# A hybrid trunk kernel: RWKV's first chunk issued at raised priority beside Mamba's end, raw weights fetched six slots ahead, two tables for the last token's shares

## The chip, the cores and the metric

The kernel runs on one core of a Trainium2 chip. The metric is the device time in microseconds (us). Several runs are timed; beside them one execution is profiled, and it has a time of its own. The engines are PE (TensorE, matrix products; PEld is its weight load), DVE (VectorE), ACT (ScalarE), POOL (GpSimd) and SP (SyncE, which here only issues DMA transfers). Each engine works through its own queue of instructions in a fixed order and waits on semaphores for the others.

## The reference

One layer over 4096 tokens of 1024 values: RMSNorm, one input projection, three groups of heads that read the same projection, one output projection, RMSNorm and the residual. The part that matters here:

```python
h = rmsnorm(x, pre_norm_w[i])
u = h @ w_in[i]
y_ssm  = mamba2_group(u[..., :SSM_IN], ...)                  # conv, SiLU, chunked scan, gate, norm
y_rwkv = rwkv7_group(u[..., SSM_IN:SSM_IN + RWKV_IN], ...)
y_mem  = memory_xattn_group(u[..., SSM_IN + RWKV_IN:], mem_k, mem_v)
y = jnp.concatenate([y_ssm, y_rwkv, y_mem], axis=-1)
x = x + rmsnorm(y @ w_out[i], post_norm_w[i])

# rwkv7_group begins with the token shift: each token takes a share of its predecessor
prev = jnp.pad(u, ((0, 0), (1, 0), (0, 0)))[:, :l, :]
us = u + (prev - u) * mu
# and its heads follow S_t = S_{t-1} (diag(w_t) + a_t^T b_t) + v_t^T k_t ; y_t = S_t r_t
```

## The kernel before, in words

The tokens are cut into 16 chunks of 256 (`NT`). The work has three phases. Phase A does the Mamba group for all chunks, phase B the RWKV group for all chunks, phase C attention and the output projection. The normalised input, transposed and split into a high and a low part (`hh`, `hl`), is written to DRAM in phase A and read again in B and C.

Every product of float32 quality is made of three matmuls on such parts: high by high, high by low, low by high. `proj_cm` (line 145) does it with the weights as the stationary operand, 24 matmuls for one block of 128 columns; a pair of blocks shares one PSUM tile `ps_pj`, of which there are two buffers. The weights are fetched raw (`fetch`, line 70, on SP's queue, into a tile `w_st`) and split by `split_w`: ACT writes `w_hi` (line 80), DVE writes `w_lo` (line 81). RWKV needs five weight blocks: the latent one `wlat` (128 columns), `wk`, `wr`, `wv` and `wg` (256 each), in four pieces each, so 20 fetches and 40 splits. `load_b` issues them, with two slots for the raw tiles.

In phase A one chunk has a stage 1 (projections, a causal convolution on DVE in `cc0` to `cc3`, lines 335 to 342) and a stage 2 (the scan in two halves: `R` holds the decays, which come back from DRAM as a broadcast, lines 386 to 438; `xdt`, `yd`, `st`, `prev`, `y`). The last chunk's stage 2 is called `a_tail`. It runs beside the beginning of phase B.

In phase B the stage 1 of a chunk calls `shifted` once for the latent block, k, r, v and g. `shifted` projects a pair of blocks into `ps_pj`, then ACT scales it by 1 - mu into `tt` (line 609), DVE adds mu times the predecessor for tokens 1 to 255 (line 610), POOL does token 0 with the table `cm`, which holds the share that the last chunk's last token left (line 612), and DVE writes the new share of this chunk's last token over it (line 613). Only after that is the PSUM buffer free for the next projection:

```python
g.tensor_tensor(out=us[:, :, 0], in0=tt[:, 0:nb, 0], in1=cm[:, m0:m0 + nb], op=ALU.add)
v.tensor_tensor(out=cm[:, m0:m0 + nb], in0=pv[:, :, NT - 1], in1=mu[:, m0:m0 + nb], op=ALU.mult)
```

The rest of stage 1 builds the products `AR` and `BK`: `lora` on the latent block (lines 642 and 643), the key norm (`norm`, line 676, with POOL's `rho`), `unit` (lines 695 to 710), `bonus` (lines 720 and 721). Then `gram2` (line 772) forms `AT`, `solve2` inverts small triangular blocks (lines 788 to 860, with `nct`, `N`, `T`, `Df`), `stage3` steps the state four times per chunk (lines 913 to 957: `UV`, `X`, `ST`, matmuls of lines 920, 927, 937), and `stage4` normalises.

What sets the order: the program is written as generators, and `weave` draws from several of them in turn, in proportion to given step counts. The result is the order of the program. The Tile framework then schedules it against a model of the engines (`schedule_with_timeline_sim=True`): instructions of a higher priority go first where they are ready, and what comes out is one fixed order per engine. The streams may be given a third number, with which `weave` issues their steps inside `tc.high_priority(offset=...)`. At the passage from A to B one line weaves the two streams:

```python
weave((a_tail, 10), (chain(load_b(), stage1(0, hT0, r0_)), 48))
```

Of the kernel before, what the change touches and what calls it, by code (L numbers as in the profile page):

```python
# [7 lines left out]
F32 = mybir.dt.float32  # L8
# [3 lines left out]
ALU = mybir.AluOpType  # L12
AX = mybir.AxisListType

P = 128
# [12 lines left out]
def tile_hymba_trunk(  # L28
# [59 lines left out]
    def load_w(src, c0, w, scale, stp, bufs=2, low=None):  # L88
        for kq in range(4):
            split_w(w, fetch(src, c0, w[0].shape[2], stp, kq, bufs), scale, kq, low)  # L90
            yield
# [443 lines left out]
    def phase_b(a_tail, a_l):  # L535
# [5 lines left out]
        ws_s = ExitStack()  # L541
        wsb = ws_s.enter_context(tc.tile_pool(name="wsb", bufs=2, side="right", reuse_waits="tile"))
        C = 64
# [5 lines left out]
        def load_b():  # L549
            for c_, w_ in ((1024, wlat), (256, wk), (0, wr), (512, wv), (768, wg)):  # L550
                yield from load_w(w2d, C_RW + c_, w_, pnc, wsb)

# [30 lines left out]
        v.memset(dcy, -0.5 * EXPM05)  # L583
        cm = bs.tile([P, 9], F32, name="cm")
        v.memset(cm, 0.0)

# [10 lines left out]
        def shifted(hT, ws, m0, nm, mid=None, pool=None, at=0, tag=None):  # L597
            wb = blocks(ws)
            nb = len(wb)
            pj = ps_pj()  # L600
            for b_ in range(nb):
# [6 lines left out]
            for b_ in range(nb):  # L608
                s.activation(out=tt[:, b_, :], in_=pv[:, b_, :], func=AF.Copy, scale=omu[:, m0 + b_:m0 + b_ + 1])
                v.scalar_tensor_tensor(out=us[:, b_, 1:NT], in0=pv[:, b_, 0:NT - 1], scalar=mu[:, m0 + b_:m0 + b_ + 1],  # L610
                                       in1=tt[:, b_, 1:NT], op0=ALU.mult, op1=ALU.add)
            g.tensor_tensor(out=us[:, :, 0], in0=tt[:, 0:nb, 0], in1=cm[:, m0:m0 + nb], op=ALU.add)
            v.tensor_tensor(out=cm[:, m0:m0 + nb], in0=pv[:, :, NT - 1], in1=mu[:, m0:m0 + nb], op=ALU.mult)  # L613
            return us
# [115 lines left out]
        r0_ = {}  # L730
        weave((a_tail, 10), (chain(load_b(), stage1(0, hT0, r0_)), 48))
        ws_s.close()
# [18 lines left out]
        v.scalar_tensor_tensor(out=amask, in0=amask, scalar=hsel[:, 1:2], in1=mk[:, 0:P], op0=ALU.max, op1=ALU.mult)  # L751
        nct = bi.tile([P, 16, 2 * NPC], F32, name="nct")
        pw = bi.tile([P, NPC, 32], F32, name="pw")
# [29 lines left out]
        def solve2(i, r):  # L783
            AT = r["AT"]
            for q in range(4):
                qs = slice(q * 32, q * 32 + 32)
                h, half = q // 2, q % 2
                s.copy(
                    out=nct[qs].rearrange("p t (c b) -> p c b t", b=2),
                    in_=AT[qs, :, h, half * 32:half * 32 + 32].rearrange("p c (b t) -> p c b t", b=2))  # L790
# [545 lines left out]
```

## Time and profile before

| | us |
|---|---|
| median of 3 runs | 2209.16 (2206.49 to 2212.63) |
| the profiled execution | 2211.41 |
| its span, first to last instruction | 2209.6 |
| PE busy | 2151.8 |
| DVE busy | 1502.7 |
| ACT busy | 1181.1 |
| POOL busy | 726.7 |
| mean granted clock of PE | 0.986 |

The span is some 1.8 us shorter than the execution's time. Busy time is the sum over an engine's instructions; matmuls are pipelined, so a busy PE is not PE at its peak. The granted clock says what share of full speed PE was given. A wait is put down to the instruction that ended last before the waiting one began. Phase A ends and phase B begins at about 740 to 800 us of the span.

### The profile page before, as it was taken

How to read it: one execution, taken by the hardware profiler on the slowest of the kernel's cores; microseconds unless marked ns; L12 is line 12 of the kernel's file. 1: busy time of each engine (PE TensorE's matmuls, PEld its weight loads, DVE VectorE, ACT ScalarE, POOL GpSimd, SP SyncE). 2: the span in 40 equal slices, each digit the busy share in tenths (PEclk: the TensorE clock that was granted, in tenths of full speed). 3: DMA queues.
4: the chain of work that ended last, by engine and by line, in shares of the span. 5: the costliest groups of instructions: out<-in, count | busy, mean ns of one | idle time of the engine just before them, and what ended most of it. 6: DMA issues, size and time to landing. Idle time of an engine off the chain costs nothing.

```text
span 2209.6 us, 50991 instructions
## 1 busy us (share of the span) xinstructions
PE 2151.8 (97%) x20705; PEld 1982.7 (90%) x20705; DVE 1502.7 (68%) x3405; ACT 1181.1 (53%) x2873; POOL 726.7 (33%) x1043
## 2 busy tenths in 40 slices
PE   8999999999999889999999999998999999999998
PEld 8999999999999788898898998987888888888986
DVE  7778788878888876577776777777573444444452
ACT  7555555555553565566666666677553333333441
POOL 2443443434433333334334333333112222222223
PEclk9999999999999999999999999999899999999999
DMA  6422233222332321111111121123243334333332
GB/s 212 148 97 87 97 134 106 97 87 96 131 109 106 118 87 40 45 64 63 50 45 45 45 83 49 45 89 129 83 172 134 125 110 162 110 133 132 100 123 77
DMA packets 82570, 218.86 MB, mean 99 GB/s; under 512 B 8151, under 2 KB 44446, under 8 KB 70046
## 3 DMA queue, kind: packets, MB, share of 16 engines
q1 hardware_dynamic: 81294, 215.59, 28.3%
q8 instruction: 163, 2.67, 0.5%
q14 instruction: 73, 0.60, 0.1%
q10 hardware_dynamic: 1040, 0.00, 0.0%
HBM read 152.00 MB, written 63.57 MB: 98 GB/s over the span
## 4 chain that ended last, share of the span: by engine, by line
PE 84%; DVE 7%; DMA 4%; ACT 3%; issue 1%; POOL 1%; SPq 0%; POOLq 0%; ACTq 0%; DVEq 0%
PE ps_pj L145 40%; PE ps_yd L155 8%; PE ps_pj L155 8%; PE ps_st L155 8%; DVE cc L338 2%; DMA R<-rowd 1%; PE ps_yd L467 1%; PE ps_yd L772 1%; PE ps_pj L1185 1%; PE ps_tr L132 1%; PE ps_yo L920 1%; PE ps_tr L1173 1%; PE ps_yo L927 1%; PE ps_st L459 1%; PE ps_yo L937 1%
## 5 line engine op out<-in xcount | busy, mean ns | idle before, releaser
L145 PE MATMUL ps_pj<-hh,w_hi 128*128 128x256 f32 x2704 | 790.5, 292 | 10.4 <-DVE cm L613 6.1
L145 PE MATMUL ps_pj<-hh,w_lo 128*128 128x256 f32 x2704 | 780.1, 289 | 0.2 <-DVE w_lo L81 0.2
L145 PE MATMUL ps_pj<-hl,w_hi 128*128 128x256 f32 x2704 | 777.2, 287 | 0.0
L145 PEld LDWEIGHTS ps_pj<-hh,w_hi 128*128 128x128 f32 x2704 | 520.2, 192 | 21.1 <-issue 6.3
L145 PEld LDWEIGHTS ps_pj<-hh,w_lo 128*128 128x128 f32 x2704 | 519.5, 192 | 6.8 <-DVE w_lo L81 0.7
L145 PEld LDWEIGHTS ps_pj<-hl,w_hi 128*128 128x128 f32 x2704 | 520.3, 192 | 5.9
L338 DVE SCALAR_TENSOR_TENSOR cc<-ux,cwh,cc 128x256 f32<-128x256 f32 x384 | 218.0, 610 | 15.4 <-ACT cc L335 15.1
L155 PE MATMUL ps_pj<-w_hi,hh 128*128 128x256 f32 (+1 forms) x528 | 155.6, 295 | 4.1 <-DVE zs L299 2.8
L155 PE MATMUL ps_pj<-w_lo,hh 128*128 128x256 f32 (+1 forms) x528 | 153.0, 290 | 0.0
L155 PE MATMUL ps_pj<-w_hi,hl 128*128 128x256 f32 (+1 forms) x528 | 152.2, 289 | 0.0
L1192 DVE TENSOR_TENSOR ya<-ps_pj,ya 64x256 f32<-64x256 f32 x64 | 26.9, 421 | 121.4 <-ACT ya L1191 121.0
L155 PEld LDWEIGHTS ps_pj<-w_hi,hh 128*128 128x128 f32 x528 | 102.1, 194 | 6.2 <-DVE zs L299 3.3
L1225 POOL TENSOR_TENSOR xr<-ot,xr 128x512 f32<-128x512 f32 x64 | 89.0, 1412 | 43.1 <-DVE ot L1224 43.1
L1219 POOL TENSOR_TENSOR sq<-sq 128x1 f32<-128x1 f32 x32 | 6.6, 207 | 292.9 <-ACT ot L1217 292.9
L155 PEld LDWEIGHTS ps_pj<-w_lo,hh 128*128 128x128 f32 x528 | 102.2, 194 | 0.3
L155 PEld LDWEIGHTS ps_pj<-w_hi,hl 128*128 128x128 f32 x528 | 102.0, 193 | 0.0
L155 PE MATMUL ps_st<-wo1l,yh 128*128 128x512 f32 x248 | 97.7, 394 | 1.0 <-DVE wo1l L1286 1.0
L155 PE MATMUL ps_yd<-wo0h,yh 128*128 128x512 f32 x248 | 98.2, 396 | 0.0
L155 PE MATMUL ps_st<-wo1h,yh 128*128 128x512 f32 x248 | 97.5, 393 | 0.0
L155 PE MATMUL ps_st<-wo1h,ylo 128*128 128x512 f32 x248 | 97.4, 393 | 0.0
L155 PE MATMUL ps_yd<-wo0h,ylo 128*128 128x512 f32 x248 | 97.3, 392 | 0.0
L155 PE MATMUL ps_yd<-wo0l,yh 128*128 128x512 f32 x248 | 97.2, 392 | 0.0
(468 smaller groups left out, 5106.8 us busy)
## 6 DMA issues: line engine op xcount, KB each, us to landing
hl<-hTd SPq DMA_DIRECT2D x32, 1024.0 KB, 5.1
hh<-hTd SPq DMA_DIRECT2D x32, 1024.0 KB, 8.3
xt<-in_x_dram SPq DMA_DIRECT2D x32, 512.0 KB, 3.5
hTd<-hh SPq DMA_DIRECT2D x16, 1024.0 KB, 6.5
hTd<-hl SPq DMA_DIRECT2D x16, 1024.0 KB, 5.5
R<-rowd SPq DMA_DIRECT2D x32, 512.0 KB, 6.6
xr<-in_x_dram SPq DMA_DIRECT2D x32, 512.0 KB, 3.9
out_dram<-xr SPq DMA_DIRECT2D x32, 512.0 KB, 2.7
```

The lines of the kernel that those rows point to most:

```text
L132: te.transpose(pt[:, q * P:(q + 1) * P], src[:, k * P:(k + 1) * P], ident)
L145: te.matmul(outp, lhsT=a[:, k, :], rhs=b[:, k, :], start=(n == 0), stop=(n == 3 * KB - 1))
L155: te.matmul(outp, lhsT=a[:, k, tsl], rhs=b[:, k, 0:ncol], start=(n == 0), stop=(n == 3 * KB - 1))
L338: v.scalar_tensor_tensor(out=cc[:, b_, :], in0=ux[:, b_, j:j + NT], scalar=wj(j), in1=cc[:, b_, :], op0=ALU.mult, op1=ALU.add)
L459: te.matmul(pst[:, gr * 256:gr * 256 + 256], lhsT=q[c]["btm"][:, gr * P:(gr + 1) * P], rhs=q[c]["xde"][:, gr * 256:gr * 256 + 256], start= ...
L467: te.matmul(yd[hf * 64:hf * 64 + 64, h * 64:h * 64 + 64], lhsT=R[:, h, hf * 64:hf * 64 + 64], rhs=xdt[:, h * 64:h * 64 + 64], start=True, ...
L772: te.matmul(pa[:, c_ * P:(c_ + 1) * P], lhsT=BK[hs, p_, c_].rearrange("p a t -> p (a t)"), rhs=AR[hs, p_, c_].rearrange("p a t -> p (a t)" ...
L920: te.matmul(pch[hs, p_ * C:p_ * C + C], lhsT=AT[:, pc, h, 0:C], rhs=UV[:, pc, h, :], start=True, stop=True)
L927: te.matmul(pch[hs, 128 + p_ * C:128 + p_ * C + C], lhsT=TT[hs, pc].rearrange("p a t -> p (a t)"), rhs=X[hs, p_, :], start=True, stop=True)
L937: te.matmul(pch[hs, 256 + p_ * C:256 + p_ * C + C], lhsT=BKt[:, pc, hs], rhs=UV[:, pc, h, :], start=True, stop=True)
L1192: v.tensor_tensor(out=ya[hs], in0=pg[hs], in1=ya[hs], op=ALU.add)
L1225: g.tensor_tensor(out=xr[:, cs], in0=ots[n_], in1=xr[:, cs], op=ALU.add)
```

## The change

There are four edits in phase B; what is computed stays the same.

1. The raw weight tiles get six slots (`wsb`, `bufs=6`), and `load_b` keeps six fetches ahead of the splits, over all five blocks in one list.
2. The stream of `load_b` and chunk 0's stage 1 is woven with a priority offset of 600 beside `a_tail`.
3. The table `cm` becomes two, `cm0` and `cm1`. A call of `shifted` reads one and writes the other, and the next call for the same columns swaps them. The writing instruction stands ahead of POOL's reading one now.
4. `nct` is no longer a tile of its own for the whole phase; each chunk's solve takes it from the one buffer that `N` uses (tag "N").

```diff
-        wsb = ws_s.enter_context(tc.tile_pool(name="wsb", bufs=2, side="right", reuse_waits="tile"))
+        wsb = ws_s.enter_context(tc.tile_pool(name="wsb", bufs=6, side="right", reuse_waits="tile"))
...
         def load_b():
-            for c_, w_ in ((1024, wlat), (256, wk), (0, wr), (512, wv), (768, wg)):
-                yield from load_w(w2d, C_RW + c_, w_, pnc, wsb)
+
+            todo = [(c_, w_, kq) for c_, w_ in ((1024, wlat), (256, wk), (0, wr), (512, wv), (768, wg)) for kq in range(4)]
+            raw = []
+            for n_ in range(len(todo) + 6):
+                if n_ >= 6:
+                    split_w(todo[n_ - 6][1], raw[n_ - 6], pnc, todo[n_ - 6][2])
+                if n_ < len(todo):
+                    c_, w_, kq = todo[n_]
+                    raw.append(fetch(w2d, C_RW + c_, w_[0].shape[2], wsb, kq, 6))
+                if n_ >= 6:
+                    yield
...
-        cm = bs.tile([P, 9], F32, name="cm")
-        v.memset(cm, 0.0)
+        cm2 = [bs.tile([P, 9], F32, name=f"cm{n_}") for n_ in range(2)]
+        v.memset(cm2[0], 0.0)
+        cms = {m0: tuple(cm2) for m0 in range(9)}
...
+            co, cn = cms[m0]
+            cms[m0] = (cn, co)
...
-            g.tensor_tensor(out=us[:, :, 0], in0=tt[:, 0:nb, 0], in1=cm[:, m0:m0 + nb], op=ALU.add)
-            v.tensor_tensor(out=cm[:, m0:m0 + nb], in0=pv[:, :, NT - 1], in1=mu[:, m0:m0 + nb], op=ALU.mult)
+            v.tensor_tensor(out=cn[:, m0:m0 + nb], in0=pv[:, :, NT - 1], in1=mu[:, m0:m0 + nb], op=ALU.mult)
+            g.tensor_tensor(out=us[:, :, 0], in0=tt[:, 0:nb, 0], in1=co[:, m0:m0 + nb], op=ALU.add)
...
-        weave((a_tail, 10), (chain(load_b(), stage1(0, hT0, r0_)), 48))
+        weave((a_tail, 10), (chain(load_b(), stage1(0, hT0, r0_)), 48, 600))
...
-        nct = bi.tile([P, 16, 2 * NPC], F32, name="nct")
...
+            nct = bi.tile([P, 16, 2 * NPC], F32, name="nct", tag="N")
```

Lines behind the edits are 9 to 13 lower in the changed kernel: its line 623 is line 610 before, 625 takes the place of 613, 690 of 677, 860 of 847, 950 of 937, 970 of 957.

The order per engine moves from Mamba's last stage on. Numbers behind names tell one buffer's uses apart. The first place is DVE's queue at the end of Mamba's last convolution. `R_9885` is the second half's decays, `cc1_10108` the last convolution block, `w_lo_10149` belongs to `wv`, `w_lo_10151` to `wg`. Before, from the arrival of `R_9885` to the end of cc1:

```order
L403 TENSOR_TENSOR de_10272<-R_9885,acs_9806 128x8
L479 SCALAR_TENSOR_TENSOR y_10006<-y_10006,sq_10073,nw_156 128x256 x2
L338 SCALAR_TENSOR_TENSOR cc1_10108<-ux1_10104,cwh_297,cc1_10108 128x256 x2
L405 TENSOR_TENSOR R_9885<-R_9885,acs_9806 128x1024
L338 SCALAR_TENSOR_TENSOR cc1_10108<-ux1_10104,cwh_297,cc1_10108 128x256 x3
L451 TENSOR_TENSOR y_10315<-ps_yo_10310,ea_9808 128x512
L338 SCALAR_TENSOR_TENSOR cc1_10108<-ux1_10104,cwh_297,cc1_10108 128x256
L438 TENSOR_TENSOR R_9885<-R_9885,ps_g_10318 128x512 x2
L342 SCALAR_TENSOR_TENSOR cc1_10108<-th_10117,cc1_10108 128x512
```

The last eleven rows of the same piece now:

```order
L81 SCALAR_TENSOR_TENSOR w_lo_10149<-w_st_10303,pnc_75,w_hi_10148 128x256 x2
L338 SCALAR_TENSOR_TENSOR cc1_10108<-ux1_10104,cwh_297,cc1_10108 128x256
L81 SCALAR_TENSOR_TENSOR w_lo_10149<-w_st_10309,pnc_75,w_hi_10148 128x256 x2
L81 SCALAR_TENSOR_TENSOR w_lo_10151<-w_st_10315,pnc_75,w_hi_10150 128x256 x2
L81 SCALAR_TENSOR_TENSOR w_lo_10151<-w_st_10321,pnc_75,w_hi_10150 128x256
L338 SCALAR_TENSOR_TENSOR cc1_10108<-ux1_10104,cwh_297,cc1_10108 128x256
L81 SCALAR_TENSOR_TENSOR w_lo_10151<-w_st_10321,pnc_75,w_hi_10150 128x256
L81 SCALAR_TENSOR_TENSOR w_lo_10151<-w_st_10340,pnc_75,w_hi_10150 128x256 x2
L338 SCALAR_TENSOR_TENSOR cc1_10108<-ux1_10104,cwh_297,cc1_10108 128x256
L81 SCALAR_TENSOR_TENSOR w_lo_10151<-w_st_10346,pnc_75,w_hi_10150 128x256 x2
L342 SCALAR_TENSOR_TENSOR cc1_10108<-th_10117,cc1_10108 128x512
```

All 40 splits now stand ahead of cc1's last instruction; from `R_9885` to it 22 wide ones and the two evictions L438 of the first half's `R_9883` stand between the old rows, where no split stood before. On SP's queue the fetch of `R_9885` stands behind 13 of the 20 weight fetches; before it stood behind 6.

The second place is DVE's queue behind the projection of r in chunk 0, `ps_pj_10549` before and `ps_pj_10550` now. `sq_10533<-ps_tr` is norm's transpose. Before:

```order
L610 SCALAR_TENSOR_TENSOR ur_10622<-ps_pj_10549,pcol_296,tt_10623 128x255
L677 STREAM_TRANSPOSE sq_10533<-ps_tr_10590 128x512
L81 SCALAR_TENSOR_TENSOR w_lo_10151<-w_st_10347,pnc_75,w_hi_10150 128x256 x2
L479 SCALAR_TENSOR_TENSOR y_10579<-y_10579,sq_10670,nw_156 128x256 x2
L610 SCALAR_TENSOR_TENSOR ur_10622<-ps_pj_10549,pcol_296,tt_10623 128x255
L81 SCALAR_TENSOR_TENSOR w_lo_10151<-w_st_10357,pnc_75,w_hi_10150 128x256 x2
L81 SCALAR_TENSOR_TENSOR w_lo_10151<-w_st_10363,pnc_75,w_hi_10150 128x256
L695 STREAM_TRANSPOSE sq_10533<-rho_10442 128x512
L81 SCALAR_TENSOR_TENSOR w_lo_10151<-w_st_10363,pnc_75,w_hi_10150 128x256
L696 TENSOR_TENSOR thw_10630<-thw_10630,sq_10533 128x512
L613 TENSOR_TENSOR cm_10186<-ps_pj_10549,pcol_296 128x2
```

And now:

```order
L623 SCALAR_TENSOR_TENSOR ur_10623<-ps_pj_10550,pcol_296,tt_10624 128x255
L690 STREAM_TRANSPOSE sq_10534<-ps_tr_10591 128x512
L451 TENSOR_TENSOR y_10580<-ps_yo_10575,ea_9808 128x512
L623 SCALAR_TENSOR_TENSOR ur_10623<-ps_pj_10550,pcol_296,tt_10624 128x255
L625 TENSOR_TENSOR cm1_10187<-ps_pj_10550,pcol_296 128x2
```

The new share is written right behind the second half of ur instead of six instructions later. PE's queue has all of r's and v's matmuls (96) ahead of norm's now; before it had norm behind 65 of them.

The third place is PE's queue at the second and third state step of chunk 0 (`ps_yo_11527` before, `ps_yo_11528` now, then `ps_yo_11748`). Before, projection matmuls follow behind the second step's last one (the first three are shown):

```order
L937 MATMUL ps_yo_11527<-UV_10846,BKt_10847 64x64 x4
L957 MATMUL ps_st_11432<-UV_10846,AT_10865 64x64 x3
L145 MATMUL ps_pj_11645<-hh_10854,w_lo_10143 128x256
L145 MATMUL ps_pj_11645<-hh_10854,w_hi_10142 128x256
L145 MATMUL ps_pj_11645<-hl_10855,w_hi_10142 128x256
```

Now the solve, the state, the norm and the third step follow, with no projection between:

```order
L950 MATMUL ps_yo_11528<-UV_10846,BKt_10847 64x64 x4
L970 MATMUL ps_st_11433<-UV_10846,AT_10865 64x64 x3
L860 MATMUL ps_g_12058<-Df_12055,AT_11434 32x32 x16
L967 MATMUL ps_yd_11432<-ST_11588,rr_10848 64x64
L967 MATMUL ps_st_11433<-ST_11588,rr_10848 64x64
L689 MATMUL ps_tr_11728<-sqh_11634,hones_10174 128x256
L689 MATMUL ps_tr_11728<-sql_11636,hones_10174 128x256
L689 MATMUL ps_tr_11728<-sqh_11634,hones_10174 128x256
L689 MATMUL ps_tr_11728<-sql_11636,hones_10174 128x256
L933 MATMUL ps_yo_11748<-UV_10846,AT_10865 64x64
```

The projections that stood there had come earlier: in the changed order chunk 0's solve begins behind k of chunk 2, before it began ahead of g of chunk 1.

## The prediction

> **What bounds the kernel now.** I read the page's first part, then the waits of PE, then the stretch where they lie, in windows of 10 us, then the instructions in order of time there.
>
> ```profile
> span 2209.6 us, 50991 instructions
> PE 2151.8 (97%) x20705; PEld 1982.7 (90%) x20705; DVE 1502.7 (68%) x3405; ACT 1181.1 (53%) x2873; POOL 726.7 (33%) x1043
> PE 84%; DVE 7%; DMA 4%; ACT 3%; issue 1%; POOL 1%; SPq 0%; POOLq 0%; ACTq 0%; DVEq 0%
> ```
>
> PE is busy for 97% and is 84% of the chain of waits. The change takes no matmul away, so it can only win back time in which PE is idle or its granted clock is low. All of the span's 57.8 us of idle PE (2209.6 - 2151.8) is not in reach either: the edits lie where Mamba ends and RWKV begins.
>
> ```profile
> 680.00:690.00 10.00, 10.00 (x85) 9.92 (x84) 7.00 (x13) 5.16 (x15) 3.39 (x5) 1.00 0.17 54
> 740.00:750.00 10.00, 7.80 (x68) 7.23 (x62) 8.80 (x19) 4.34 (x13) 2.26 (x4) 1.00 0.52 169
> 750.00:760.00 10.00, 5.78 (x34) 4.71 (x35) 9.23 (x19) 5.78 (x13) 1.86 (x3) 0.83 0.65 245
> 760.00:770.00 10.00, 8.01 (x72) 7.00 (x71) 9.88 (x28) 6.21 (x16) 5.80 (x6) 0.83 0.30 79
> 770.00:780.00 10.00, 9.40 (x64) 8.11 (x65) 9.36 (x19) 7.56 (x21) 3.16 (x5) 0.66 0.40 103
> 790.00:800.00 10.00, 3.89 (x21) 3.72 (x20) 8.64 (x16) 3.77 (x8) 7.66 (x9) 0.70 0.21 54
> 830.00:840.00 10.00, 7.24 (x186) 6.87 (x185) 7.63 (x16) 5.46 (x13) 7.78 (x7) 0.75 0.01 2
> 840.00:850.00 10.00, 10.00 (x113) 9.37 (x112) 6.10 (x12) 2.74 (x7) 1.23 (x2) 0.91 0.40 147
> 900.00:910.00 10.00, 6.82 (x63) 5.69 (x63) 7.80 (x26) 6.92 (x17) 3.24 (x6) 0.66 0.08 28
> sum 280.00, PE 258.83 PEld 240.46 DVE 209.27 ACT 159.87 POOL 101.87; mean PE 9.24 PEld 8.59 DVE 7.47 ACT 5.71 POOL 3.64
> ```
>
> The columns are the window, its length, then busy us of PE, PEld, DVE, ACT and POOL, the granted clock, the DMA share and GB/s. From 680 to 960 us PE is idle for 280 - 258.83 = 21.2 us. The clock falls right behind each cluster of idle time: a row at 0.66 has lost 10 x (1 - 0.66) = 3.4 us of work, if PE had work. The low rows add up to 16.6 us, so some 38 us is the ceiling of a gain. And from 740 to 780 us DVE is busy for 37.3 of 40 us: **there DVE is the bound, not PE.** The change adds nothing to DVE and takes nothing from it; it changes the order.
>
> ```profile
> PE ps_pj L145 <- DVE cm L613: 6.1, 1, 6.1
> PE ps_pj L145 <- ACT cc L335: 2.7, 1, 2.7
> PE ps_tr L416 <- ACT btm L423: 2.6, 1, 2.6
> PE ps_yd L957 <- DVE cm L613: 1.4, 1, 1.4
> PE ps_g L847 <- DVE Df L841: 1.4, 1, 1.4
> PE ps_g L835 <- ACT pw L830: 1.3, 1, 1.3
> SPq L70 <- DVE w_lo L81: 34.0, 14, 5.9
> ```
>
> These are the waits in that stretch (us in total, times, longest). The last row is the two slots: 14 fetches waited 34.0 us for a split.
>
> **First term: the weights ahead of Mamba's last block.** The order rows show 22 of the 32 wide splits between the second R and the end of cc1, where before there were none, and the two evictions of the first R (L438) too. What that costs:
>
> ```profile
> 744.35 0.40 SPq L386 DMA_DIRECT2D R<-rowd  x1
> 751.12 0.17 DVE L403 TENSOR_TENSOR de<-R,acs 128x8 f32<-128x8 f32 x1 [0.76 <-DMA R<-rowd]
> 758.13 0.68 DVE L342 SCALAR_TENSOR_TENSOR cc<-th,cc 128x512 f32<-128x512 f32 x1
> 758.73 0.87 DVE L81 SCALAR_TENSOR_TENSOR w_lo<-w_st,pnc,w_hi 128x256 fp32r<-128x256 f32 x2
> 777.99 0.39 PE L145 MATMUL ps_pj<-hh,w_hi 128*128 128x256 f32 x1
> L81 DVE SCALAR_TENSOR_TENSOR w_lo<-w_st,pnc,w_hi 128x256 fp32r<-128x256 f32 x32 | 17.0, 561 | 3.6 <-ACT w_hi L80 3.5
> L438 DVE TENSOR_TENSOR R<-R,ps_g 128x512 f32<-128x512 f32 x4 | 2.6, 679 | 0.0
> ```
>
> R was issued at 744.35 and DVE took it up at 751.12; cc1 ended at 758.81, 7.7 us later. Now 13 fetches stand ahead of this R in SP's queue instead of 6, and the last of them waits for a split of wk; DVE comes to that split about 1 us later than to the one that held the queue before (bounds 0 to 3). From there to the end of cc1 DVE does the old 7.7 us, two L438 (2 x 0.65 = 1.3 us) and 22 splits of 17.0/32 = 0.53 us, 11.7 us. So cc1 ends at 752.1 + 7.7 + 1.3 + 11.7 = 772.8 instead of 758.8, and its transposes hold PE's queue that long: PE has only 96 projection matmuls (11.5 us at the 0.12 of the second term) and a few small ones ahead of them from 740 us on.
>
> Behind cc1 it is given back in part. From 758.8 to 777.99, where PE begins the r projection and is dense from then on, DVE did 14 splits, 14 x 0.53 = 7.4 us, which are done by now: 772.8 + 19.2 - 7.4 = 784.6. **The r projection starts 6.6 us later** (the same as 1 + 1.3 + 8 splits of 0.53). Bounds: the pair of splits at 758.73 took 0.87 us, which gives 8 x 0.43 and 5.7 us in all; with R 3 us later and splits of 0.56, their mean when timed one by one, it is 8.8.
>
> **Second term: the wait on cm.**
>
> ```profile
> 789.04 2.95 POOL L679 TENSOR_TENSOR rho<-rho,mhalf 128x16 f32<-128x16 f32 x1
> 796.48 0.15 DVE L613 TENSOR_TENSOR cm<-ps_pj,pcol 128x2 f32<-128x2 f32 x1
> 796.77 0.55 PE L145 MATMUL ps_pj<-hh,w_hi 128*128 128x256 f32 x1 [6.11 <-DVE cm L613]
> 740.45 0.28 PE L145 MATMUL ps_pj<-hl,w_hi 128*128 128x256 f32 x1
> 740.57 0.28 PE L145 MATMUL ps_pj<-hh,w_lo 128*128 128x256 f32 x1
> ```
>
> cm overwrote the table that POOL still had to read; POOL stood in rho (2.95 us), so cm sat behind six other instructions, and with it the PSUM slot of the next projection. With two tables it stands right behind the second ur. The 6.1 us go, and so do 2 us of half clock behind the wait (in the row at 0.70 PE worked for 3.89 us, nearly all of it at half clock). What is late next: the same DVE queue now holds norm's transpose ahead of ur's second half, and PE issues norm only behind all 96 matmuls of r and v (96 x 0.12 us, from the two rows 740.45 and 740.57, is 11.5 us). From norm to cm DVE has four instructions, about 2 us, in which PE waits. And PE's long idle time before 784 puts a low clock over the start of r: 0 to 3.4 us by the row at 0.66, of which I take half, 1.7, since the sparse time itself covers the rest. Together -6.1 - 2.0 + 2.0 + 1.7 = **-4.4 us** (bounds -6.1 and -2.7).
>
> **Third term: chunk 1 and the solve.** PE runs further ahead of DVE now (g, the next latent block and k of chunk 1 without a break). It meets the products BK and the slot of k before DVE is done: two waits of the kind of the 1.4 and 1.7 us rows, **+2 us** (0 to 4). In return the solve of chunk 0 comes only behind k of chunk 2, interleaved with projections, so the 1.3 and 1.4 us of L835 and L847 are covered, and so is the low clock behind them (rows 830 and 840: 2.5 and 0.9 us): **-6.1 us** (0 to -6.1). The second wait on cm, 1.4 us, goes as well, less some 0.5 us for L937 standing bare: **-0.9 us.**
>
> **Fourth term: the recurrence without filling.** The solve that was put off meets chunk 0's state steps. The order rows show two steps in a row without one projection between them. Such a bare stretch is the row 900:910: 3.2 us idle and 3.4 us of clock, 6.6 of 10. In the new one the solve's and norm's small matmuls stand between the hops, so I take **+5 us** (3 idle, 2 clock; bounds 0 and 13, two full stretches).
> By the Trainium skill (TensorE: Matmul & The Clock Gate, Part 1) the clock is halved only behind an idle window of about 3.4 us, so gaps of 1 us would not lower it and this term would be 3, the sum 2 us lower. The trace disagrees: the row at 0.75 stands behind gaps of 1.3 and 1.4 us.
>
> What costs nothing: the larger pool and the buffer that nct shares with N. One chunk's N is read out long before the next chunk's copies, and where nct does wait, the projections of the chunk behind it keep PE at work; without that cover it would be one solve's wait per chunk, which the dense rows do not let me see. From chunk 3's latent block on the two orders are within some ten matmuls of each other. From RWKV's end to attention the order differs in small pieces: 0, bounds -4 and +4.
>
> **Sum:** 6.6 - 4.4 + 2 - 6.1 - 0.9 + 5 = +2.2 us. On the profiled execution's own 2211.4 us (its span and 1.8 us around it) that is 2213.6; this execution is 2.3 us above the median of the runs, 2209.2, so I predict **2211 us**, no change that a measurement of this kernel can tell (0.3%, 6.6 us).
>
> **The rivals.** A: the front gains. The bare stretch is filled, splits cost what an undisturbed pair shows, no low clock falls on r, chunk 1 does not wait: 5.7 - 6.1 - 2.0 + 2.0 + 0 - 6.1 - 0.9 = -7.4, and -11 with a kind turn into attention: about 2200. For it: 38 us stand open and the three longest waits are all here. Against it: DVE was busy for 37.3 of 40 us where the front begins, so it can't start sooner than DVE allows.
> B, slower: the recurrence packed bare. Two stretches like 900:910 instead of my 5 us, 13.2 us, with all else as above: 2211 + 8 = 2219. It decides when the filling between two hops of a state step is shorter than the hop, 1.3 us or so; the trace has one such stretch already, and the rows of order have a second with even less between.
> That the change does nothing is excluded by the order rows on every engine; that its parts cancel is the forecast.
>
> **How the numbers follow.** The forecast (within 0.3%) 0.44, A 0.30, B 0.26; the chances of faster, the same and slower are these. The likeliest case's own range is 2204 to 2217. The range that holds 8 in 10 takes in A and B with the turn into attention: 2197 to 2224.
>
> **What would show it.** Right: cc1's last L342 near 773 us with PE idle before it for about 8 us; the r projection near 785; no wait on cm; one of about 2 us behind norm; rows L835 and L847 without idle time. Wrong: cc1 before 766 (DVE not the bound), or PE idle by more than 8 us between 860 and 910 (B), or the clock at 1.00 from 785 to 900 (A).

## The result

| | before | after |
|---|---|---|
| median, us | 2207.61 (2206.49 to 2212.63, 5 runs) | 2229.26 (2227.78 to 2234.27, 5 runs) |
| the profiled execution, us | 2211.41 | 2227.78 |
| its span, us | 2209.6 | 2226.1 |
| PE busy, us | 2151.8 | 2163.1 |

The changed kernel is slower: the ratio is 1.010, with a 95% interval of 1.0084 to 1.0116. By medians that is 21.7 us, by the two profiled executions 16.4 us; the one of before lay 3.8 us above its median, the one of after 1.5 us below. The prediction was 2211 us, no change. The ratios, here and below, are not those of the medians and can stand a little off them.

From the page of the kernel after, its span, its busy times and its chain of waits by engine:

```profile
span 2226.1 us, 51064 instructions
PE 2163.1 (97%) x20705; PEld 1993.2 (90%) x20705; DVE 1503.6 (68%) x3405; ACT 1183.5 (53%) x2873; POOL 714.5 (32%) x1043
PE 87%; DVE 4%; ACT 3%; DMA 3%; issue 2%; POOL 1%; POOLq 0%; SPq 0%; DVEq 0%; ACTq 0%
```

PE has the same 20705 matmuls and works 11.3 us longer on them; its idle time grew from 57.8 to 63.0 us. The waits of PE from 735 to 930 us (total, times, longest):

```profile
PE ps_g L436 <- DVE R L438: 4.7, 1, 4.7
PE ps_pj L145 <- DVE cm L625: 3.5, 3, 2.0
PE ps_tr L416 <- DVE cc L342: 2.1, 1, 2.1
PE ps_yo L933 <- ACT UV L926: 1.6, 1, 1.6
PE ps_yo L940 <- ACT X L936: 1.2, 2, 0.8
PE ps_yo L950 <- ACT UV L945: 0.8, 1, 0.8
```

The wait of 6.1 us on cm is gone. Mamba's end waits instead (R, cc), and so do the hops of the state steps (UV, X).

**Where the time went.** The same piece of work can be laid side by side in both executions. I use three: the *front*, to the first matmul of chunk 4's latent block; the *dense stretch*, from chunk 5's nct to chunk 14's; and the *turn*, from there to attention. The columns of the windows are those of the prediction. The front's last part, from the first r matmul of chunk 0 to chunk 4's latent block, and in it the part from chunk 2's first r matmul to chunk 3's, then the dense stretch and the turn; before:

```profile
778.00:943.40 165.40, 153.35 (x1855) 143.10 (x1854) 114.61 (x294) 99.88 (x241) 58.43 (x80) 0.94 0.16 54
861.60:917.20 55.60, 52.42 (x673) 47.09 (x671) 39.45 (x118) 32.99 (x83) 17.24 (x25) 0.94 0.12 44
1049.48:1468.84 419.36, 419.36 (x5691) 377.37 (x5690) 300.37 (x793) 278.05 (x685) 161.96 (x217) 1.00 0.15 54
1468.84:1760.00 291.16, 278.48 (x2442) 247.64 (x2442) 174.47 (x402) 153.23 (x395) 63.79 (x103) 0.96 0.37 127
```

and after:

```profile
780.70:950.70 170.00, 156.08 (x1856) 144.87 (x1855) 108.18 (x279) 93.38 (x228) 60.22 (x81) 0.94 0.12 43
857.50:925.50 68.00, 60.78 (x855) 54.14 (x855) 44.29 (x128) 38.63 (x97) 20.33 (x27) 0.90 0.10 37
1056.58:1480.85 424.27, 424.27 (x5686) 381.76 (x5687) 306.64 (x793) 279.25 (x685) 155.63 (x217) 1.00 0.15 53
1480.85:1776.40 295.55, 281.10 (x2440) 249.34 (x2440) 172.97 (x403) 156.25 (x398) 61.82 (x104) 0.97 0.37 127
```

Up to 720 us the two run the same order, and this execution of after is 2.3 us ahead at 710 us (2.5 at 720, so the marks hold to some 0.2 us). Its r starts at 780.70 instead of 777.99, so 5.0 us late on that clock; r to chunk 4 takes 4.6 us more. By the first row of each view PE is idle for 1.9 us more there (12.05, then 13.92) and busy for 2.7 us more, with the same matmuls to one and the same granted clock of 0.94. **The front lost 9.6 us, the dense stretch 4.9, the turn 4.4.** With the 2.3 us ahead and 0.2 between, that is the 16.4 us of the two executions. In the dense stretch PE is busy for 100% in both, with the same matmuls to within five, and still a chunk takes 47.1 us after and 46.6 before.

### The profile page after: what moved, and what is told of

The parts are those of the page before. It is cut to its first block, busy times and chain, and to the rows that moved or that the text cites. A ratio compares the mean times of both kernels' runs of the same rounds, so it can differ in the third digit from the quotient of the medians.

```text
span 2226.1 us, 51064 instructions
## 1 busy us (share of the span) xinstructions
PE 2163.1 (97%) x20705; PEld 1993.2 (90%) x20705; DVE 1503.6 (68%) x3405; ACT 1183.5 (53%) x2873; POOL 714.5 (32%) x1043
## 4 chain that ended last, share of the span: by engine, by line
PE 87%; DVE 4%; ACT 3%; DMA 3%; issue 2%; POOL 1%; POOLq 0%; SPq 0%; DVEq 0%; ACTq 0%
PE ps_pj L145 41%; PE ps_pj L155 8%; PE ps_yd L155 8%; PE ps_st L155 8%; PE ps_yd L467 1%; PE ps_pj L1198 1%; PE ps_tr L132 1%; PE ps_yo L933 1%; PE ps_tr L1186 1%; PE ps_st L459 1%; PE ps_st L784 1%; DVE cc L338 1%; PE ps_yo L446 1%; PE ps_yo L950 1%; DMA w_st<-in_w_out_dram 1%
## 5 line engine op out<-in xcount | busy, mean ns | idle before, releaser
L145 PE MATMUL ps_pj<-hh,w_hi 128*128 128x256 f32 x2704 | 789.4, 292 | 3.9 <-DVE cm L625 3.5
L145 PE MATMUL ps_pj<-hh,w_lo 128*128 128x256 f32 x2704 | 778.9, 288 | 0.0
L145 PE MATMUL ps_pj<-hl,w_hi 128*128 128x256 f32 x2704 | 778.0, 288 | 0.0
L145 PEld LDWEIGHTS ps_pj<-hh,w_hi 128*128 128x128 f32 x2704 | 520.2, 192 | 14.5 <-ACT tt L622 3.1
L145 PEld LDWEIGHTS ps_pj<-hl,w_hi 128*128 128x128 f32 x2704 | 520.0, 192 | 7.8
L145 PEld LDWEIGHTS ps_pj<-hh,w_lo 128*128 128x128 f32 x2704 | 519.6, 192 | 5.9
```

What stands on the lines that cost most here:

```text
L145: te.matmul(outp, lhsT=a[:, k, :], rhs=b[:, k, :], start=(n == 0), stop=(n == 3 * KB - 1))
```

## The experiments

The front of an experiment is given as the start of chunk 4's latent block against before, less what the execution was off at 710 to 720 us; a chunk's length as the mean from chunk 5's nct to chunk 14's. The difference of medians is against before on the same chip.

| run | medians, us | ratio (interval) | front, us | us a chunk |
|---|---|---|---|---|
| six slots alone | +2.5 | 1.001 (0.9998 to 1.0021) | -0.4 | 46.60 |
| raised priority alone | +12.4 | 1.0061 (1.0043 to 1.0079) | +9.1 | 46.61 |
| two tables alone | +0.8 | 1.0004 (0.9995 to 1.0013) | -4.7 | 47.21 at the end |
| shared nct alone | -0.4 | 1.0005 (0.9994 to 1.0015) | -1.5 | 46.59 |
| all but the priority | +9.7 | 1.004 (1.0022 to 1.0057) | +2.2 | 47.14 |
| all but the tables | +14.7 | 1.0071 (1.0056 to 1.0087) | +8.5 | 47.30 |
| all but the slots | +20.8 | 1.01 (1.0083 to 1.0118) | +7.5 | 47.14 |
| all but the shared nct | +25.7 | 1.0118 (1.0099 to 1.0137) | +8.2 | 47.16 |
| tables in chunks 0 and 1 | -7.8 | 0.9965 (0.9954 to 0.9976) | -6.0 | 46.46 |
| tables in chunk 0 | +6.4 | 1.0023 (1.001 to 1.0035) | -2.5 | 47.16 |
| all edits, tables in chunks 0 and 1 | +6.8 | 1.0033 (1.0019 to 1.0046) | +8.1 | 46.35 |
| raised weights alone | -3.7 | 0.9991 (0.998 to 1.0002) | -0.5 | 46.61 |
| raised weights, tables in chunks 0 to 2 | -9.5 | 0.995 (0.9931 to 0.9969) | -8.1 | 46.46 |
| slots, nct, tables in chunks 0 and 1 | -3.4 | 0.9976 (0.9965 to 0.9988) | -1.3 | 46.35 |

### Each edit alone

Theory 1 was the prediction's first term: the splits ahead of Mamba's last block. Theory 2 put the loss behind it.

**Six slots.** The edit is that of the diff, `bufs=6` and the new `load_b`, on the kernel before.

> Only edit 1, six slots for the raw weights; one table, no raised priority, nct as before. In its order all 24 splits that stood behind cc1's last instruction stand ahead of it, as in the changed kernel. Theory 1 (the splits ahead of Mamba's last block cost the time): cc1 ends 8 to 14 us later than before, the r projection 5 to 7 us later, and the whole kernel is 6 to 10 us slower, about 2216 us. Theory 2 (the time is lost behind it, in the order of the dense stretch and of the turn into attention): the late start is caught up by 920 us, since the splits are done by then, and the kernel is within 3 us of before.

The waits of PE in it that changed, 735 to 930 us:

```profile
PE ps_tr L416 <- DVE cc L342: 5.2, 1, 5.2
PE ps_pj L145 <- DVE cm L622: 3.7, 2, 3.6
```

cc1's last L342 was late by 10 us, and r started 4.9 us late; but at chunk 2's r this kernel was 3.9 us ahead, and the whole differs by nothing that can be told (the interval ends at 1.0021, 4.6 us). Theory 1 fell: the splits have to be done at some time, and done early they shorten what follows.

**Raised priority.**

```diff
-        weave((a_tail, 10), (chain(load_b(), stage1(0, hT0, r0_)), 48))
+        weave((a_tail, 10), (chain(load_b(), stage1(0, hT0, r0_)), 48, 600))
```

> Only edit 2, the raised priority. Two splits instead of none stand between the second R and the end of cc1. Theory 1: without the six slots there is little to move ahead, cc1 ends 1 to 2 us later, the kernel is within 3 us of before. Theory 2: the order behind it differs too, so 0 to 4 us slower. More than 6 us slower would say that the raised priority itself, by letting the projections run ahead of the state steps, is what costs.

12.4 us slower, which neither theory had expected. PE's waits in it, 735 to 930 us:

```profile
PE ps_pj L145 <- DVE cm L613: 13.6, 2, 8.7
PE ps_g L436 <- DVE de L403: 4.3, 1, 4.3
PE ps_pj L642 <- DVE lt L626: 4.2, 1, 4.2
```

The waits on cm grew from 6.1 and 1.4 us to 13.6, and two waits of over 4 us are new. The front is 9.1 us late, 2.4 of it at r and the rest behind.

**Two tables**, with four constant tiles `w0h`, `a0h`, `kah`, `kai` packed into one for room.

```diff
+            co, cn = cms[m0]
+            cms[m0] = (cn, co)
...
-            g.tensor_tensor(out=us[:, :, 0], in0=tt[:, 0:nb, 0], in1=cm[:, m0:m0 + nb], op=ALU.add)
-            v.tensor_tensor(out=cm[:, m0:m0 + nb], in0=pv[:, :, NT - 1], in1=mu[:, m0:m0 + nb], op=ALU.mult)
+            v.tensor_tensor(out=cn[:, m0:m0 + nb], in0=pv[:, :, NT - 1], in1=mu[:, m0:m0 + nb], op=ALU.mult)
+            g.tensor_tensor(out=us[:, :, 0], in0=tt[:, 0:nb, 0], in1=co[:, m0:m0 + nb], op=ALU.add)
```

> Only edit 3, the two tables; four small constant tiles are packed into one to make room. Mamba's end is in the old order. Theory 1: the 6.1 us wait on cm and the low clock behind it go and little comes in its place, so 4 to 8 us faster, about 2203 us. Theory 2: its order in the dense stretch and at the turn into attention is close to the changed kernel's, so the gain at 796 us is there in the trace but is lost again behind 1040 us (0.5 us a chunk, and some 4 us at the turn), and the kernel is within 4 us of before or slower.

The front gained 4.7 us, as both had it, and the whole nothing, as theory 2 had it: from chunk 9 on each chunk took 47.21 us. The 4 to 8 us of theory 1 did not come.

**Shared nct**, the last edit of the diff alone.

> Only edit 4, nct in N's buffer. Theory 1 and the prediction: nothing, within 2 us of before. Theory 2, if the shared buffer is what makes each chunk 0.45 us longer in the dense stretch (47.1 us from one chunk's nct to the next one's, before 46.7) and disturbs the last two solves: 5 to 9 us slower.

No change. The edit is free, as predicted.

### Each edit taken out

Theory P: the raised priority costs the front. Theory I: the parts cost only together.

**Without the raised priority**, against the changed kernel:

```diff
-        weave((a_tail, 10), (chain(load_b(), stage1(0, hT0, r0_)), 48, 600))
+        weave((a_tail, 10), (chain(load_b(), stage1(0, hT0, r0_)), 48))
```

> The changed kernel without edit 2, the raised priority; six slots, two tables and nct in N's buffer stay. Theory P (the raised priority costs the time at Mamba's end and in the first chunks: alone it was 12 us slower, and its trace lost 8 to 9 us from 740 to 920 us): the stretch 740 to 1040 us comes out about 4 us shorter than before, the dense stretch 1040 to 1480 us 5 us longer (as with the two tables alone), the whole within 4 us of before, about 2207 us, some 20 us faster than the changed kernel. Theory I (the parts are harmless alone and cost together, splits ahead of cc1 with two tables): still 8 us or more slower than before.

**With one table:** the lines of `cm2`, `co` and `cn` go back to

```diff
+            g.tensor_tensor(out=us[:, :, 0], in0=tt[:, 0:nb, 0], in1=cm[:, m0:m0 + nb], op=ALU.add)
+            v.tensor_tensor(out=cm[:, m0:m0 + nb], in0=pv[:, :, NT - 1], in1=mu[:, m0:m0 + nb], op=ALU.mult)
```

> The changed kernel with one table again; six slots, raised priority and nct in N's buffer stay. Theory P: waits on cm of some 13 us come back as with the raised priority alone, the dense stretch 1040 to 1480 us takes its old time (46.7 us a chunk instead of 47.1); together 8 to 14 us slower than before, about 2216 us. Theory I: with the table's wait back the projections don't run ahead of the state steps, no bare stretches, within 5 us of before.

**With two slots**, and the old `load_b`:

```diff
-        wsb = ws_s.enter_context(tc.tile_pool(name="wsb", bufs=6, side="right", reuse_waits="tile"))
+        wsb = ws_s.enter_context(tc.tile_pool(name="wsb", bufs=2, side="right", reuse_waits="tile"))
```

> The changed kernel with two slots again and the old order of the fetches; raised priority, two tables and nct in N's buffer stay. Theory P: the loss stays, 10 to 18 us slower than before, since the splits ahead of cc1 cost nothing in the run with six slots alone. Theory I: without the splits ahead of cc1 the loss in the stretch 740 to 920 us goes, and what is left is the 5 us of the dense stretch less the 4 us of the table's wait: within 4 us of before.

**With an nct of its own**, the constants packed for room:

```diff
+        nct = bi.tile([P, 16, 2 * NPC], F32, name="nct")
...
-            nct = bi.tile([P, 16, 2 * NPC], F32, name="nct", tag="N")
```

> The changed kernel with nct as a tile of its own again; room for it comes from packing four small constant tiles into one. Both theories: the same as the changed kernel within 3 us, 18 to 23 us slower than before, since nct in N's buffer alone changed nothing. If the turn into attention (1480 to 1680 us) comes out 5 us or more shorter, the shared buffer is what made it long in the changed kernel.

Without the raised priority the front's loss fell from 9.6 to 2.2 us and the whole from 21.7 to 9.7, so the priority is the largest part; but it stayed 9.7 us slower, where P had said 4 at most and I 8 or more. The other three kept both the priority and a front of +7.5 to +8.5. Without the slots and without the shared nct the loss, 20.8 and 25.7 us, was above the 18 and 23 forecast at most. With one table the waits on cm came back (9.1 us in total) and the loss went by only 7 us. What P and I had both missed is in the last column: in all four a chunk takes 47.1 to 47.3 us, with one table too. So it isn't the second table's writing that costs there.

### The order that the dense stretch settles into

In PE's queue the order of one chunk repeats itself exactly from chunk to chunk once the start is over. There are two such cycles here: A, in the kernel before and in the runs with slots, priority or nct alone, and B, in the changed kernel, in all four runs with one edit taken out, and from chunk 9 on with the two tables alone. Two kernels tell the cycle from the table: one uses two tables in chunks 0 and 1 and keeps A; the other uses them in chunk 0 alone and falls into B.

```diff
+            turn_[m0] = turn_.get(m0, 0) + 1
+            cms[m0] = (cn, co) if turn_[m0] < 2 else (cn, cn)
```

> Edit 3 alone, but with two tables only in chunks 0 and 1; from chunk 2 on one table is read and overwritten as before. Up to chunk 3 PE's order is that of the two tables alone; behind it each chunk repeats the order of the kernel before (cycle A), where with the two tables throughout, and in the changed kernel, each chunk repeats another one (cycle B). Theory C (the order that the dense stretch settles into costs 0.45 us a chunk; the table itself costs nothing): the front keeps the gain of 4 to 5 us, the distance from one chunk's nct to the next one's is 46.7 us to the end instead of 47.1, and the kernel is 3 to 6 us faster than before, about 2200 us. Theory W (the second table's write in each chunk costs, whatever the order): the gain of the front is kept too, since the writes are gone from the dense stretch, and the two theories are told apart by the next run.

(`< 1` in the second. In both, and in every kernel below with two tables in the first chunks alone, POOL's reading instruction stands first again, as before.)

> The same with two tables in chunk 0 alone. There is one table less in use than in the last run, but the order settles into cycle B from chunk 6 on. Theory C: 47.1 us a chunk from there, some 4 to 5 us slower than with two chunks of two tables, so within 3 us of before. Theory W: 46.7 us a chunk, the same time as with two chunks.

The dense stretch of the first, and of the second:

```profile
1045.00:1463.13 418.13, 418.13 (x5690) 376.30 (x5690) 300.27 (x793) 277.75 (x684) 161.96 (x217) 1.00 0.15 54
```

```profile
1048.54:1472.98 424.44, 424.44 (x5686) 382.25 (x5687) 306.27 (x793) 277.58 (x684) 155.36 (x217) 1.00 0.15 53
```

With less of the second table the dense stretch took 6.3 us more. In cycle B a chunk takes 47.14 us with two tables throughout (the changed kernel) and 47.16 with one. Theory C holds and W falls: **the time goes with the cycle, not with the table.** The first of the two is 7.8 us faster than before, where 3 to 6 had been forecast; the second is 6.4 us slower, where it was to stay within 3.

How much of that is the order's? I added up the time from each matmul's start to the next one's over the nine chunks, apart for the projections (L145) and for all other matmuls. The others take 160.0 to 160.2 us in all ten runs of cycle A and 164.5 to 164.8 in all six of cycle B, so **the cycle costs 0.5 us a chunk.** The projections take 257.1 to 259.3 us in A and 259.7 to 261.0 in B. In A they differ between kernels with the same PE order (it is why the table has 46.35, 46.46 and 46.59), so something other than that order sets them too; what it is was not tried.

What makes B longer shows first in the products of L772 (now L784), whose two halves go to `ps_yd` and `ps_st`. In a dense chunk before, eight of them (start, duration, line, tiles):

```profile
1180.97 0.37 PE L772 MATMUL ps_yd<-AR,BK 64*128 64x128 f32 x1
1180.99 0.37 PE L772 MATMUL ps_st<-AR,BK 64*128 64x128 f32 x1
1181.19 0.27 PE L772 MATMUL ps_yd<-AR,BK 64*128 64x128 f32 x1
1181.20 0.27 PE L772 MATMUL ps_st<-AR,BK 64*128 64x128 f32 x1
1181.30 0.27 PE L772 MATMUL ps_yd<-AR,BK 64*128 64x128 f32 x1
1181.31 0.27 PE L772 MATMUL ps_st<-AR,BK 64*128 64x128 f32 x1
...
1181.42 0.27 PE L772 MATMUL ps_st<-AR,BK 64*128 64x128 f32 x1
```

and in a dense chunk after:

```profile
1188.77 0.71 PE L784 MATMUL ps_yd<-AR,BK 64*128 64x128 f32 x4
...
1190.46 0.27 PE L784 MATMUL ps_st<-AR,BK 64*128 64x128 f32 x1
1190.57 0.27 PE L784 MATMUL ps_yd<-AR,BK 64*128 64x128 f32 x1
1190.58 0.61 PE L784 MATMUL ps_st<-AR,BK 64*128 64x128 f32 x4
```

Two matmuls of different halves start 0.01 us apart, and the next pair 0.11 us later (0.21 behind the first pair). Four of one half in a row take such a step each. Over the nine chunks a half follows itself 18 times before and 72 times after, and the time from each of these matmuls' starts to the next matmul's start adds up to 26.96 us before and 29.22 after. That is 2.3 of the 4.4 us that the small matmuls lost. The first products of the state steps (L920, now L933) lost as much, 13.74 to 16.00. The rest comes out even: norm, the transposes of BK and L954 take 1.4 to 1.7 us more each, bonus, lora and two parts of the solve 1.2 to 1.9 less.

### The raised priority, and what beats both

**All edits, two tables in chunks 0 and 1 only**: the changed kernel's front with another cycle.

> The changed kernel, all four edits, but two tables only in chunks 0 and 1. PE's order is the changed kernel's through the first state steps, then cycle A and another order of the turn into attention. Theory C: the 10 to 12 us of the front stay lost, the 5 us of the dense stretch and some of what the turn cost come back: 8 to 12 us slower than before instead of 21, about 2215 us. If it stays 18 us or more slower, the front alone makes the changed kernel's loss.

A came back (46.35 us a chunk), the front stayed lost (+8.1), 6.8 us slower.

**The raised priority for the weights alone**: `load_b` is stepped inside the raised priority, `stage1` is not.

```diff
+        def lifted(gen):
+            while True:
+                with tc.high_priority(offset=600):
+                    if next(gen, gen) is gen:
+                        return
+                yield
...
-        weave((a_tail, 10), (chain(load_b(), stage1(0, hT0, r0_)), 48))
+        weave((a_tail, 10), (chain(lifted(load_b()), stage1(0, hT0, r0_)), 48))
```

> The kernel before with the raised priority for the weight loads alone; chunk 0's stage 1 keeps the common priority. Its splits stand as in the kernel before, none between the second R and cc1. Theory P1 (what costs 12 us when the whole stream is raised is chunk 0's stage 1 ahead of Mamba's last steps): within 3 us of before. Theory P2 (the raised weights cost): 6 us or more slower.

P1 holds: -3.7 us instead of +12.4. **What costs is chunk 0's stage 1 at raised priority.** In the table every run that has it has a front of +7.5 to +9.1 us, with one table or two, two slots or six; no run without it is above +2.2. It was not run without the raised weights beside it.

Open was how it costs. The waits on cm don't explain it: they grew by 6.1 us where it stood alone, but by only 1.6 in the run with all but the tables (9.1 us against 7.5), where the front lost nearly as much. With two tables, the order lets the projections run ahead: in the traces the first four state steps (L920) stand in PE's queue behind 448, 489, 558 and 600 of RWKV's projection matmuls before, and behind 580, 600, 600 and 651 in the changed kernel. Two kernels vary that, and the kernel before was profiled again. The first joins `lifted(load_b())` with the line of the two tables at `< 3`; the second is the changed kernel with that line at `< 2` and the weave without 600. The counts in the two texts below are not those of the traces, where the first kernel has 454, 480, 536 and 592, and the second 500, 573, 600 and 641.

```diff
+            cms[m0] = (cn, co) if turn_[m0] < 3 else (cn, cn)
...
+        weave((a_tail, 10), (chain(lifted(load_b()), stage1(0, hT0, r0_)), 48))
```

> Raised priority for the weight loads alone and two tables in chunks 0 to 2; two slots, chunk 0's stage 1 at the common priority, nct as before. In its order the first seven state steps begin behind 400, 436, 509, 536, 600, 632 and 727 matmuls of RWKV's projections (before: 407, 458, 520, 563, 600, 632, 727; changed kernel: 528, 528, 550, 600, 600, 600, 715), and the dense stretch is cycle A. Theory F (the changed kernel's front loses where state steps follow each other without projections between): from the first r matmul of chunk 2 to that of chunk 3 it takes 55 to 57 us as before, where the changed kernel took 68.0, and with the table's gain it is 5 to 10 us faster than before, about 2199 us. Theory T (two tables together with any raised priority make the front lose): 60 us or more in that stretch, and not faster than before.

> Six slots, nct in N's buffer, two tables in chunks 0 and 1, no raised priority. State steps begin behind 479, 528, 547, 600, 600, 600 and 715 projection matmuls, three of them at one place; the dense stretch is cycle A. Theory F: the stretch from chunk 2's first r matmul to chunk 3's takes 61 to 66 us, and the kernel is 2 to 6 us slower than before, some 5 us faster than with the two tables throughout (cycle B), which was 10 us slower. Theory T: without a raised priority the front loses nothing, so as fast as before or faster.

> The kernel before itself, for a second profiled execution of the same order. If the turn into attention (1480 to 1680 us) shows fewer than two windows of half clock, the first profile's 20 us of half clock there were one execution's, and the changed kernel's turn is to be compared with this one: then its loss there is 8 to 10 us and not 4. If it shows 20 us again, the turn of the changed kernel cost 4 us.

The same windows for the one with raised weights and tables in chunks 0 to 2:

```profile
773.90:936.20 162.30, 155.79 (x1858) 143.85 (x1858) 114.10 (x303) 102.73 (x250) 60.01 (x83) 0.96 0.18 58
858.10:910.10 52.00, 50.68 (x664) 46.24 (x662) 36.91 (x115) 32.58 (x81) 17.69 (x25) 0.93 0.13 47
```

for the one with slots, nct and tables in chunks 0 and 1:

```profile
784.30:943.90 159.60, 151.68 (x1853) 141.33 (x1853) 108.16 (x280) 93.09 (x226) 57.70 (x80) 0.97 0.13 46
858.20:918.10 59.90, 54.88 (x720) 49.15 (x719) 41.97 (x126) 35.93 (x93) 18.31 (x27) 0.94 0.11 41
```

and for the one with all edits and tables in chunks 0 and 1, which differs from the last in the raised priority alone:

```profile
860.20:926.80 66.60, 58.94 (x855) 52.54 (x854) 43.37 (x126) 38.06 (x95) 19.23 (x27) 0.90 0.10 37
```

The first holds for F and against T: tables and a raised priority together, no step put off, 52.0 us, and 9.5 us faster than before. The second went against F's price: 59.9 us where F had 61 at least, and 3.4 us faster than before, not slower. But it is not the case that F speaks of: in its trace no three steps stand at one place. In the third kernel's they do (580, 600, 600, 600), and there the stretch takes 66.6 us. Set beside the third, one thing is clear: with the raised stage 1 the first step stands behind 580 projections instead of 500, the stretch holds 855 matmuls instead of 720, with the same 216 projections among them, and it takes 6.7 us more, at a granted clock of 0.90 instead of 0.94. The 135 others are done earlier in the second kernel, and even so its way from r to chunk 2's r is 3.9 us shorter (73.9 us against 77.8). I read that as put-off small matmuls with too little between them; that the clustering itself is the cause was argued from the order, not isolated. One run speaks against it: with all edits but the slots, the first steps stand behind 504, 588, 600 and 628, no two at one place, and the front lost 7.5 us. So which run has the loss is shown; how the raised stage 1 makes it stays open.

The second profile of before has a turn of the first one's kind, with clocks of 0.74 and 0.83 in the same two windows:

```profile
1540.00:1560.00 20.00, 18.48 (x324) 16.43 (x322) 10.06 (x25) 13.10 (x32) 1.48 (x4) 0.74 0.10 32
1580.00:1600.00 20.00, 17.63 (x165) 15.72 (x165) 11.80 (x29) 10.14 (x30) 1.53 (x4) 0.83 0.42 146
```

So the changed kernel's turn took 4.4 us more than this order's first profile. But with nct shared alone, whose PE order there is before's, the turn took less:

```profile
1466.94:1752.00 285.06, 272.91 (x2442) 242.53 (x2442) 175.11 (x402) 153.48 (x395) 63.66 (x103) 0.99 0.38 129
```

That is 6.1 us less than before, at a clock of 0.99 instead of 0.96, and yet its median is before's. Why the clock differs there stays open, and 4.4 us can't be called the edits' where one order differs by 6.1. The changed kernel's own waits from 1480 to 1720 us begin with these; the one of 3.3 us is in the runs with all but the slots and all but the shared nct too, and in no other:

```profile
PE ps_yd L970 <- DVE UV L945: 3.9, 2, 3.3
PE ps_st L155 <- ACT wo1h L1298: 2.2, 1, 2.2
PE ps_yo L933 <- ACT UV L926: 1.5, 1, 1.5
PE ps_g L1168 <- ACT TT L877: 1.4, 1, 1.4
```

**The version that beats both** is the one with raised weights alone and two tables in chunks 0 to 2: 2197.29 us, 0.995 of before (0.9931 to 0.9969), with two slots and an nct of its own.

## Why the prediction was wrong

**First term, weights ahead of Mamba's last block (+6.6 at r): right in kind, a little large.** The rows of after on DVE:

```profile
749.43 0.16 DVE L403 TENSOR_TENSOR de<-R,acs 128x8 f32<-128x8 f32 x1
766.34 0.68 DVE L342 SCALAR_TENSOR_TENSOR cc<-th,cc 128x512 f32<-128x512 f32 x1
```

From R's arrival to the end of the last L342 it is 17.6 us, where I had 7.7 + 1.3 + 11.7 = 20.7. The splits cost some 0.39 us each beside each other, less than my lower bound of 0.43. r came 5.0 us late. That the slots make this delay is shown by the run with slots alone (+4.9); that the delay is made up for by the end is shown by the same run, as far as its interval tells.

**Second and third term, the wait on cm, chunk 1 and the solve (-9.4 together): right in kind, too large.** The wait of 6.1 us went, one of 2.0 us stands behind norm, and the solve's two waits are gone; the low clock that I put on r did not come (it was 1.00 from 780.70 to 795.40 us). The parts from r to chunk 2's r and from there to chunk 4's latent block, before and then after:

```profile
778.00:861.60 83.60, 74.73 (x795) 71.79 (x794) 62.17 (x146) 50.41 (x117) 30.25 (x40) 0.92 0.23 77
861.60:943.40 81.80, 78.62 (x1063) 71.31 (x1062) 52.44 (x149) 49.47 (x124) 28.18 (x40) 0.96 0.09 31
780.70:857.50 76.80, 70.10 (x621) 67.31 (x619) 50.87 (x121) 38.38 (x89) 29.41 (x40) 0.96 0.17 63
857.50:950.70 93.20, 85.98 (x1237) 77.55 (x1237) 57.31 (x159) 55.00 (x140) 30.81 (x42) 0.93 0.08 27
```

To chunk 2's r the idle time fell by 2.2 us, and the clock's loss from 6.8 to 3.4 us (half clock for 13.7 us, then for 6.8): 5.6 us won, not 9.4. By position the sum to there was 6.6 - 4.4 + 2 - 6.1 - 0.9 = -2.8 and -1.8 was measured, but that is luck: the changed kernel stands there with 174 matmuls fewer behind it (621 against 795).

**Fourth term, the recurrence without filling (+5, bounds 0 and 13): the mechanism was seen, its size was too small.** From chunk 2's r to chunk 4's latent block the idle time grew by 4.0 us and the clock's loss by 3.4, 7.4 together. Rival B had the kind, but its 13.2 was too large. The stretch is 11.4 us longer, and the rest of that is the put-off matmuls themselves. I also had no line for the part of the edit that does it, the priority of stage 1, apart from the weights.

**A term that I did not have:** from r to chunk 4 PE is busy 2.7 us longer on the same matmuls. My sum counted idle time and clock alone.

**The step that failed outright: "from chunk 3's latent block on the two orders are within some ten matmuls of each other", taken as no cost.** The positions were close; the order inside a chunk was another cycle, and the stretch came out 4.9 us longer over nine chunks, 4.4 of it in the small matmuls that the cycle reorders. A count of positions cannot show that, and since PE is busy for 100% in both, no row of idle time could either.

**The turn, 0 with bounds of 4:** 4.4 us, just outside, and less than the 6.1 us between two executions of one PE order there.

nct and the larger pool at 0 were right, by the two runs alone. On the profiled execution's own time the forecast was 2213.6 and the time 2227.8. The 14.2 us between are 7.4 of the front (3.8 of the second and third term, 2.4 of the fourth, 2.7 of busy time, less 1.6 of the first, to 0.1), 4.9 of the dense stretch and 4.4 of the turn, less the 2.5 us by which phase A and the piece ahead of the dense stretch ran shorter. The base was 2.3 us high as well, which I took off; after's execution then lay 1.5 us below its own median.

## What to carry to other kernels

Where a static scheduler orders a long loop, compare the order of one steady chunk before and after, not positions: an edit at the loop's start can move the whole loop into another cycle, and a PE busy for 100% hides what that costs. Raise only what is late (here the weights), not the stream behind it: here that lost 7.5 to 9.6 us at the front in every kernel that did it. And try an edit alone and for a few iterations only: the two tables gained where the wait was, and kept on throughout they led the loop into the dearer cycle.

## What the runs showed of the hardware

Matmuls of 64 rows on different halves of the array start in pairs, 0.01 us apart, so that eight of 64x128 take some 0.55 us from the first start to where a ninth would stand (1180.97 to 1181.42, and a step of 0.11); on one half in a row they are 0.11 us or more apart, and no pair forms. The Trainium skill (TensorE: Matmul & The Clock Gate, Part 3) says that matmuls on different row groups overlap with some 4 ns between their starts; the trace agrees in kind, with 10 ns. I had not expected that the order alone, with no idle time and the clock at 1.00, is worth 1% of a dense stretch: 4.4 us of 419, all in the small matmuls (160.1 us in cycle A, 164.5 in B). Nor had I expected that the 1944 projection matmuls of the stretch take 257.1 us in one kernel and 259.3 in another with the same PE order; why is open.
